# Pair 0's scores among the gate products, roots behind its exponentials, one masked copy per head with differences of value blocks, and another order of the projections

## The chip, the cores and the metric

One core of one Trainium2 chip runs the kernel. The metric is the device time of one execution in microseconds. The kernel before takes 871.64 us (median of three runs, 871.32 to 872.03). Its engines are named as in the profile: PE (TensorE matmuls), PEld (its weight loads), DVE (VectorE), ACT (ScalarE), POOL (GpSimd), SP (SyncE, which here only issues DMAs).

## The reference

One layer of a decoder on 512 tokens of width 1024, all float32: an FFN half step, a mixer, another FFN half step, each with an RMS norm on both sides. The mixer is what matters here.

```python
def rg_lru(x_in, conv_w, conv_b, w_rg, b_rg, w_ig, b_ig, lam):
    xc = causal_depthwise_conv(x_in, conv_w, conv_b)
    r = jax.nn.sigmoid(block_diag(xc, w_rg, b_rg).astype(jnp.float32))
    i = jax.nn.sigmoid(block_diag(xc, w_ig, b_ig).astype(jnp.float32))
    log_a = LRU_C * r * jax.nn.log_sigmoid(lam.astype(jnp.float32))
    a = jnp.exp(log_a)
    mult = jnp.sqrt(-jnp.expm1(2.0 * log_a))
    u = mult * (i * xc.astype(jnp.float32))
...
    _, h = lax.associative_scan(combine, (a, u), axis=1)
...
    scores = jnp.where(mask[None, :, None, None], scores, MASK_VALUE)
    sink = sinks.astype(jnp.float32).reshape(1, 1, N_KV_HEADS, GQA_GROUP, 1, 1)
    m = jnp.maximum(jnp.max(scores, axis=-1, keepdims=True), sink)
    p = jnp.exp(scores - m)
    denom = jnp.sum(p, axis=-1, keepdims=True) + jnp.exp(sink - m)
    p = (p / denom).astype(v.dtype)
    out = jnp.einsum("bnkgqj,bnjkd->bnqkgd", p, v_band)
...
    y_lru = rg_lru(x_lru, conv_w, conv_b, w_rg, b_rg, w_ig, b_ig, lam) * jax.nn.gelu(gate_lru)
    y_attn = sliding_window_sink_attention(q, k, v, sinks)
    y = jnp.concatenate([rms_norm(y_lru, g_lru_out), rms_norm(y_attn, g_attn_out)], axis=-1)
    return y @ w_o
```

The attention has 8 query heads of 64 over 2 key heads, with a window of 128: a query sees its own block of 128 keys up to itself, and of the block before only the keys behind its own place. So for each place in a block exactly one of the two blocks' keys counts, and a head's weights of one query block fit in one 128x128 tile.

## The kernel before

Each float32 product is made of three passes over parts of lower precision: every operand is split into a high part (a cast on ACT) and a low part (a subtraction on DVE), and hi*hi + hi*lo + lo*hi are accumulated in PSUM. Weights are loaded in pieces of 1 MB into five raw buffers (`raw_`) by SP, cast to `whi_` on ACT (line 172) and subtracted to `wlo_` on DVE (line 177). A class `Weights` holds a list of weight units in their order of use. `take` hands out the next one; `cast(n)` puts the casts of the next n on ACT's queue, `fill(n)` their subtractions too, and when a raw buffer's last unit is subtracted the next load goes to SP. The order of all work is the order in which the program text issues it (no scheduler): each engine has one queue and works it off in order, waiting where an operand isn't there.

The program is FFN 1, a boundary (norms and transposes, in which the four products `an` of the recurrence's input are made), the mixer, a second boundary, FFN 2. In the mixer 24 matmuls (eight steps of three) make each further projection: `pk`, `pv`, four `pq` (one per pair of heads; pair j is heads j and j + 4, called n = 0 and 1) and four `gt` (the recurrence's GELU gates). A projection is made in one go by `in_product`, or bit by bit by `pump(n)`, which puts n steps of the next projection in PE's queue between other work.

The recurrence, per 128 of 512 channels (ci = 0 to 3): a convolution (ACT and DVE, `xc`), its split, gate products `rg` and `ig` (six matmuls a ci), sigmoids and tanh (ACT), `decay_a` (exp on ACT, a square `m` on POOL), `decay_b` (DVE), `root` (square root on ACT), `root_u` (a product, on POOL for ci 0 and 1, on DVE for 2 and 3), `scan` (DVE), and at the end a product with the GELU of `gt` (`gelu_a` to `gelu_d`, a copy on DVE, then square and tanh on ACT between DVE steps).

The attention, per pair: `products` (scores `sc` on PE in four PSUM banks, line 1340), `scores` (mask and maximum on DVE, lines 1346 to 1352), `exps` (ACT, line 1361), `normalise` (DVE, line 1368), `turn_p` (transposes on PE, line 1376, a copy `pa` on ACT), masked copies `pc` on POOL (lines 1385 and 1386: for each head four selects, which part a block into its own keys and those of the block before), `values` (products with v on PE, line 1394), `rows_high` and `rows_low` (the split of the result, ACT and DVE). Here pair 0's scores stand behind all gates, pq0, the transposes of v and three steps of pq1; its mask and exponentials stand behind all decays and roots. For j = 1 to 3 a loop puts the values of pair j - 1 in PE's queue, the scores, exponentials and normalisation of pair j on DVE and ACT, five steps of a projection on PE, then pair j's transposes and the scores of pair j + 1.

After the loop the products with w_o follow. Their row scales need the mean squares of both halves (`balance`, which sums on PE the `acc_lru` and `acc_attn` of DVE).

## Time and profile before

| | us |
|---|---|
| median of three runs | 871.64 (871.32 to 872.03) |
| the profiled execution | 869.65, its span 867.9 |
| PE busy | 847.4 (98%) |
| DVE busy | 657.3 (76%) |
| ACT busy | 527.4 (61%) |
| POOL busy | 173.9 (20%) |
| mean granted clock of PE | 0.996 |

The span runs from the first to the last instruction of the profiled execution; the execution's time also has what lies around it. Busy is the sum of an engine's instructions. Matmuls overlap each other, so PE can be busy without being at its peak. A row of a group of instructions names line, engine, operation, output and inputs and shapes, then the count, the busy time in us, the mean of one in ns, and the time that its engine idled before it with what ended the idling.

### The profile page before, as it was taken

What the parts mean: (1) busy time and instruction counts of PE and PEld (TensorE: products, weight loads), DVE (VectorE), ACT (ScalarE), POOL (GpSimd) and SP (SyncE); (2) the same over time, 40 slices, a digit from 0 to 9 for tenths busy, and PEclk for the clock granted to TensorE, in tenths of its full rate; (3) what the DMA queues carried; (4) which work ended last, traced back from release to release, by engine and by line L of the source; (5) the groups of instructions that cost most, each with busy time, mean ns of one, the idle gap of its engine ahead of it and who ended that gap; (6) DMA issues with size and microseconds to landing.
All of it is one profiled execution on the core that took longest, in us unless ns stands there. A gap on an engine that the chain in (4) does not pass through costs nothing.

```text
span 867.9 us, 14095 instructions
## 1 busy us (share of the span) xinstructions
PE 847.4 (98%) x5502; PEld 768.3 (89%) x5502; DVE 657.3 (76%) x898; ACT 527.4 (61%) x896; POOL 173.9 (20%) x211
## 2 busy tenths in 40 slices
...
GB/s 244 98 194 194 146 100 233 178 115 232 116 136 288 125 211 77 91 56 48 82 65 122 64 35 290 74 108 207 120 95 101 237 154 132 233 98 188 262 85 97
DMA packets 92902, 124.42 MB, mean 143 GB/s; under 512 B 5864, under 2 KB 62500, under 8 KB 92836
## 3 DMA queue, kind: packets, MB, share of 16 engines
...
q10 hardware_dynamic: 144, 0.13, 0.0%
...
## 4 chain that ended last, share of the span: by engine, by line
PE 85%; DVE 7%; ACT 4%; DMA 2%; issue 1%; SPq 0%; POOL 0%; DVEq 0%; ACTq 0%
PE aa L820 12%; PE ab L820 11%; PE da L820 6%; PE db L820 5%; PE ba L820 3%; PE wo L1602 3%; PE bb L820 3%; PE an L702 1%; PE mn L702 1%; PE yal L1148 1%; PE yal L1149 1%; PE yal L1147 1%; PE yb L1149 1%; PE yb L1147 1%; PE yb L1148 1%; DMA raw_second<-in_ffn_w_gu 1%
## 5 line engine op out<-in xcount | busy, mean ns | idle before, releaser
L928 POOL DMA_DIRECT2D yp_b<-stage x42 | 36.5, 1111 | 149.7 <-ACT stage L925 144.2
L928 POOL DMA_DIRECT2D yp_a<-stage x42 | 37.0, 1135 | 146.5 <-ACT stage L925 141.2
...
L1147 PE MATMUL yal<-whi_ad,hha 128*128 128x512 f32 x48 | 18.9, 393 | 0.0
L1149 PE MATMUL yal<-whi_ad,hla 128*128 128x512 f32 x48 | 18.7, 390 | 0.0
L1148 PE MATMUL yal<-wlo_ad,hha 128*128 128x512 f32 x48 | 18.7, 389 | 0.0
L1147 PE MATMUL yb<-whi_bd,hhb 128*128 128x512 f32 x48 | 18.7, 389 | 0.0
L1148 PE MATMUL yb<-wlo_bd,hhb 128*128 128x512 f32 x48 | 18.7, 389 | 0.0
L1149 PE MATMUL yb<-whi_bd,hlb 128*128 128x512 f32 x48 | 18.7, 389 | 0.0
L177 DVE TENSOR_TENSOR wlo_bd<-raw_bd,whi_bd 128x1024 fp32r<-128x1024 f32 x10 | 12.1, 1223 | 8.1 <-ACT whi_bd L172 8.1
L1291 POOL TENSOR_TENSOR xcl<-xc,xch 128x512 fp32r<-128x512 f32 x4 | 6.9, 1754 | 54.5 <-ACT xch L1290 54.5
L1385 POOL TENSOR_SCALAR_AFFINE_SELECT pc<-pa 128x256 f32<-128x256 f32 x16 | 10.8, 676 | 32.3 <-ACT pa L1378 32.3
L177 DVE TENSOR_TENSOR wlo_ad<-raw_ad,whi_ad 128x1024 fp32r<-128x1024 f32 x10 | 12.2, 1221 | 4.0 <-ACT whi_ad L172 4.0
L177 DVE TENSOR_TENSOR wlo_wo<-raw_wo,whi_wo 128x1024 fp32r<-128x1024 f32 x8 | 10.0, 1256 | 6.7 <-ACT whi_wo L172 6.5
L1268 DVE SCALAR_TENSOR_TENSOR xc<-an,cols,xc 128x511 f32<-128x511 f32 (+2 forms) x12 | 8.2, 742 | 9.0 <-ACT xc L1264 9.0
L553 POOL TENSOR_TENSOR xg_f<-xh_f,xl_f 128x256 f32<-128x256 f32 x8 | 5.8, 759 | 42.2 <-DVE xl_f L484 42.2
L410 PE MATMUL pq<-xh_mx,whi_q 128*128 128x512 f32 x32 | 13.6, 425 | 0.0
L603 ACT ACTIVATE sqxr<-x_rows 128x512 f32<-128x512 f32 x16 | 10.0, 631 | 5.6 <-DVE x_rows L633 5.6
L1682 POOL TENSOR_TENSOR yp_b<-yp_b,grow 128x512 f32<-128x512 f32 x6 | 7.8, 1292 | 27.2 <-ACT ysq L1675 27.0
L1148 PE MATMUL ybl<-wlo_bd,hhb 128*128 128x512 f32 (+1 forms) x36 | 13.2, 366 | 0.0
L1147 PE MATMUL ybl<-whi_bd,hhb 128*128 128x512 f32 (+1 forms) x36 | 13.2, 366 | 0.0
L1149 PE MATMUL ybl<-whi_bd,hlb 128*128 128x512 f32 (+1 forms) x36 | 13.2, 365 | 0.0
...
## 6 DMA issues: line engine op xcount, KB each, us to landing
...
```

The costliest lines, as they stand in the source:

```text
L177: low.tensor_sub(two(lo, x), x, two(hi.bitcast(F32), x))
L410: pe.matmul(ps, hi[:, k, :], xh, start=start, stop=False)
L603: act.activation(wt(f"sq{name}{self.name}{tb}{dh}"), src, AF.Square, accum_out=self.ss[name, tb][:, dh:dh + 1])
L702: pe.matmul(b[:, l], w[part][:, k, :], xs[k][xpart][:, l], start=k + part + xpart == 0, stop=stop and k == KD - 1)
L820: pe.matmul(o, w[:, k, js], x, start=first and i + j + k == 0, stop=k == 3 and i == 2, skip_group_check=True)
L928: pool.dma_start(o, st.rearrange("p (a b) -> p a b", a=2) if len(o.shape) == 3 else st, accum_op=ALU.add)
L1147: pe.matmul(ps, hh[:, blk], hi[:, k, cs], start=start, stop=False)
L1148: pe.matmul(ps, hh[:, blk], lo[:, k, cs], start=False, stop=False)
L1149: pe.matmul(ps, hl_[:, blk], hi[:, k, cs], start=False, stop=stop)
L1268: dve.scalar_tensor_tensor(o, xl_banks[ci][:, :T - back], col("conv_w", (CONV - 1 - back) * KC + ci), o, op0=ALU.mult, op1=ALU.add)
L1385: pool.affine_select(t[:, :, 0, :], cur, pattern=[[0, 2], [1, P]], base=0, channel_multiplier=-1, compare_op=ALU.is_ge, fill=0.0)
L1602: pe.matmul(wo_banks[tb][dh], x, w[:, k, :], start=start and k == 0 and w is hi and not xp, stop=stop and k == 1 and xp == 1, skip_group_c ...
```

## The change

- Projections are made in another order: pk, pq0, pv, pq1, pq2, gt0, pq3, gt1, gt2, gt3 (before pk, pv, pq0, pq1, gt0, pq2, pq3, gt1, gt2, gt3), and the weights' list and casts follow. All four `conv_a` stand together.
- Pair 0's score products stand between the gate products of ci 1 and ci 2; its mask and maximum follow the gates; then pv, its exponentials, pq1 with the transposes of v inside, its normalisation. `decay_a` comes behind its exponentials, `decay_b` and the roots behind its transposes and the scores of pair 1.
- Per head one select instead of four makes `pc`, of blocks 1 to 3 alone; `pa` stays as the other operand. With vd, the difference of each value block to the one before, a block's own part is pc times vd, and the block behind takes pa times v without a mask. `values` has 12 matmuls instead of 8, for the same columns.
- `root_u` is on DVE for all ci. The copy of `gt` is on ACT instead of DVE, right after its product.
- In the loop a pair's fill is 9, 9 and 10 steps before its transposes instead of 5, and root products, scans and GELU steps stand behind `rows_low`.
- The means (`balance`) come one weight's products later among those of w_o.

PE's queue around pair 0's scores, before (`ig` and `rg` gate products, `vt` the transposes of v, `pq` pq1, `sc` the scores):

```order
L412 MATMUL ig_4490<-xch_4380,lo_w_ig 128x512
L1477 MATMUL vt<-ident,vT 128x128 x4
L410 MATMUL pq_4515<-xh_mx_3694,whi_q_4358 128x512
L411 MATMUL pq_4515<-xl_mx_3695,whi_q_4358 128x512
L412 MATMUL pq_4515<-xh_mx_3694,wlo_q_4359 128x512
L410 MATMUL pq_4515<-xh_mx_3696,whi_q_4358 128x512
L411 MATMUL pq_4515<-xl_mx_3697,whi_q_4358 128x512
L412 MATMUL pq_4515<-xh_mx_3696,wlo_q_4359 128x512
L410 MATMUL pq_4515<-xh_mx_3698,whi_q_4358 128x512
L411 MATMUL pq_4515<-xl_mx_3699,whi_q_4358 128x512
L412 MATMUL pq_4515<-xh_mx_3698,wlo_q_4359 128x512
L1340 MATMUL sc_4526<-kTh,qT0h 128x128
```

and now, where they begin:

```order
L409 MATMUL rg_4433<-xch_4353,lo_w_rg 128x512
L407 MATMUL ig_4434<-xch_4353,hi_w_ig 128x512
L408 MATMUL ig_4434<-xcl_4354,hi_w_ig 128x512
L409 MATMUL ig_4434<-xch_4353,lo_w_ig 128x512
L1338 MATMUL sc_4449<-kTh,qT0h 128x128
L1338 MATMUL sc_4451<-kTh,qT0h 128x128
L1338 MATMUL sc_4449<-kTl,qT0h 128x128
```

The score products stand between two sets of gates (24 score products, then the gates of ci 2 and 3); pv and pq1, 48 matmuls, come behind the second set and ahead of the transposes of pair 0. Before, all gates, the transposes of v and nine matmuls of pq1 stood ahead of them.

DVE's queue between pair 2's normalisation (`sc`) and the low part of pair 3's queries (`qT3l`), which the score products of pair 3 need. Before, pair 2's normalisation is followed by it at once:

```order
L1366 TENSOR_TENSOR den_4931<-den_4931,es_4932 128x4
L1367 RECIPROCAL den_4931<-den_4931 128x4
L1368 TENSOR_TENSOR sc_4933<-sc_4933,den_4931 128x512
L1366 TENSOR_TENSOR den_4947<-den_4947,es_4948 128x4
L1367 RECIPROCAL den_4947<-den_4947 128x4
L1368 TENSOR_TENSOR sc_4949<-sc_4949,den_4947 128x512
L1316 TENSOR_TENSOR qT3l<-pq_4827,qT3h 128x512
L484 SCALAR_TENSOR_TENSOR yal_4956<-po_4914,cols,yah_4955 128x512
```

and now (`yal` and `acc_attn` are pair 1's result and its sum of squares, `xc` the recurrence's input, `gq` its GELU):

```order
L1366 TENSOR_TENSOR sc_4898<-sc_4898,den_4896 128x512
L481 SCALAR_TENSOR_TENSOR yal_4918<-po_4904,cols,yah_4917 128x512
L1410 TENSOR_TENSOR acc_attn<-acc_attn,sq_a_4920 128x512
L1305 TENSOR_TENSOR xc_4314<-xc_4314,th_4489 128x512
L1305 TENSOR_TENSOR xc_4316<-xc_4316,th_4504 128x512
L1308 SCALAR_TENSOR_TENSOR xc_4312<-r_4441,xc_4312 128x512
L1424 SCALAR_TENSOR_TENSOR gq_4860<-gq_4860,gt_4858 128x512
L1314 TENSOR_TENSOR qT3l<-pq_4862,qT3h 128x512
```

Six instructions, two of them root products (`xc<-xc,th`), one a scan (`xc<-r,xc`), stand ahead of the low part.

ACT's queue at the same place, before (`yah` the high part of the result, `pa` the copy of the transposes, `whi_` casts of weights):

```order
L1361 ACTIVATE sc_4949,den_4947<-sc_4866,nm_4945 128x128
L481 ACTIVATE yah_4955<-po_4914,cols 128x512
L441 ACTIVATE sq_a_4958<-po_4914 128x512
L172 CAST whi_wo_4967<-raw_wo_4893 128x1024
L1315 CAST qT3h<-pq_4827 128x512
L1378 COPY pa_4995<-pt_4990 128x512
L1378 COPY pa_5011<-pt_5006 128x512
```

and now:

```order
L1359 ACTIVATE sc_4898,den_4896<-sc_4820,nm_4894 128x128
L478 ACTIVATE yah_4917<-po_4904,cols 128x512
L438 ACTIVATE sq_a_4920<-po_4904 128x512
L172 CAST whi_gt_0_4928<-raw_gt__4846 128x1024
L1427 ACTIVATE gq_4860<-gq_4860 128x512
L1313 CAST qT3h<-pq_4862 128x512
L1376 COPY pa_4975<-pt_4970 128x512
L1376 COPY pa_4987<-pt_4982 128x512
```

The tanh of the first GELU (`gq<-gq`), which needs the DVE step quoted above, stands ahead of the high part `qT3h` and of pair 2's copies.

The diff (cut where it only renames or follows from the rest):

```diff
@@ -306,11 +305,9 @@
-    for add in (q[0], q[1], gt[0], q[2], q[3], *gt[1:]):
+    for add in (kv[0], q[0], kv[1], q[1], q[2], gt[0], q[3], *gt[1:]):
         add()
     WO = [(k, dh) for k in (KC, KC + 2, 0, 2) for dh in range(2)]
 ...
@@ -1257,11 +1254,12 @@
     xcs, th, rs_, us_ = [], [], [], []
-    def conv(c0):
-        for ci in (c0, c0 + 1):
-            xcs.append(t2k(f"xc{ci}"))
-            act.activation(xcs[ci], xl_banks[ci], AF.Identity, bias=col("conv_b", ci), scale=col("conv_w", 3 * KC + ci))
+    def conv_a(ci):
+        xcs.append(t2k(f"xc{ci}"))
+        act.activation(xcs[ci], xl_banks[ci], AF.Identity, bias=col("conv_b", ci), scale=col("conv_w", 3 * KC + ci))
+    def conv_b(c0):
         for back in range(1, CONV):
             for ci in (c0, c0 + 1):
                 o = xcs[ci][:, back:]
@@ -1304,7 +1302,7 @@
         act.activation(th[ci], th[ci], AF.Sqrt)
     def root_u(ci):
-        (pool if ci < 2 else dve).tensor_mul(us_[ci], us_[ci], th[ci])
+        dve.tensor_mul(us_[ci], us_[ci], th[ci])
     def scan(ci):
         dve.tensor_tensor_scan(hl[ci], rs_[ci], us_[ci], initial=0.0, op0=ALU.mult, op1=ALU.add)
@@ -1374,25 +1372,28 @@
         for b in range(NB):
             bs = slice(b * P, (b + 1) * P)
             pe.transpose(pt[:, bs], p[:, bs], ident)
-        pa = wt(f"pa{j}{n}")
+        pa, pc = (t2k(f"{t}{j}{n}") for t in ("pa", "pc"))
         act.copy(pa, pt)
-        pairs = unit[j, n] = [t2k(f"pc{j}{n}{i}") for i in range(2)]
-        for i, t in enumerate(pairs):
-            t = t.rearrange("p (b w k) -> p b w k", b=2, w=2)
-            cur = v4(pa)[:, 2 * i:2 * i + 2, :]
-            pre = v4(pa)[:, 2 * i + 1:min(2 * i + 3, NB), :]
-            nb = 2 - i
-            pool.affine_select(t[:, :, 0, :], cur, pattern=[[0, 2], [1, P]], base=0, channel_multiplier=-1, compare_op=ALU.is_ge, fill=0.0)
-            pool.affine_select(t[:, :nb, 1, :], pre, pattern=[[0, nb], [-1, P]], base=0, channel_multiplier=1, compare_op=ALU.is_gt, fill=0.0)
+        pool.affine_select(v4(pc)[:, 1:, :], v4(pa)[:, 1:, :], pattern=[[0, NB - 1], [1, P]], base=0, channel_multiplier=-1, compare_op=ALU.is_ge, fill=0.0)
+        unit[j, n] = pa, pc
     def values(j):
         o = bank(f"po{j}")
         for b in range(NB):
-            w = P if b == NB - 1 else 2 * P
             for n in range(2):
-                pe.matmul(o[n * HD:(n + 1) * HD, b * P:b * P + w], v[:, b * P + n * HD:b * P + (n + 1) * HD],
-                          unit[j, n][b // 2][:, 2 * (b % 2) * P:2 * (b % 2) * P + w], start=b == 0, stop=b == NB - 1, skip_group_check=True)
+                pa, pc = unit[j, n]
+                chans = slice(b * P + n * HD, b * P + (n + 1) * HD)
+                keys, own = slice(b * P, min(b + 1 + (not b), NB) * P), slice(b * P, (b + 1) * P)
+                if b:
+                    pe.matmul(o[n * HD:(n + 1) * HD, own], vd[:, chans], pc[:, own], start=False, stop=b == NB - 1, skip_group_check=True)
+                else:
+                    pe.matmul(o[n * HD:(n + 1) * HD, keys], v[:, chans], pa[:, keys], start=True, stop=False, skip_group_check=True)
+            for n in range(2):
+                pa, pc = unit[j, n]
+                chans, nxt = slice(b * P + n * HD, b * P + (n + 1) * HD), slice((b + 1) * P, (b + 2) * P)
+                if 0 < b < NB - 1:
+                    pe.matmul(o[n * HD:(n + 1) * HD, nxt], v[:, chans], pa[:, nxt], start=False, stop=False, skip_group_check=True)
         po[j] = o
     def rows_high(j):
@@ -1414,7 +1415,8 @@
     def gelu_a(ci):
         b = gts[ci]
-        gts[ci] = taken(wt(f"gt{ci}"), b)
+        gts[ci] = wt(f"gt{ci}")
+        act.copy(gts[ci], b)
         gqs[ci] = t2k(f"gq{ci}")
         act.activation(gqs[ci], gts[ci], AF.Square, scale=(GC * GA) ** 0.5)
 ...
@@ -1441,12 +1444,11 @@
         yield
     def fill_steps():
-        yield from in_steps("pq1", lambda b: q_parts(1, b), 1)
-        yield from in_steps("gt0", lambda b: gelu(0, b), 0)
-        for j in (2, 3):
-            yield from in_steps(f"pq{j}", lambda b: q_parts(j, b), 0)
+        yield from in_steps("pq2", lambda b: q_parts(2, b))
+        yield from in_steps("gt0", lambda b: gelu(0, b))
+        yield from in_steps("pq3", lambda b: q_parts(3, b))
         for ci in range(1, KC):
-            yield from in_steps(f"gt{ci}", lambda b: gelu(ci, b), 0)
+            yield from in_steps(f"gt{ci}", lambda b: gelu(ci, b))
     steps = fill_steps()
@@ -1454,96 +1456,102 @@
         for _ in range(n):
             next(steps, None)
-    conv(0)
-    pk = in_product("pk", (), 1)
+    for ci in range(KC):
+        conv_a(ci)
+    conv_b(0)
+    pk = in_product("pk", (), 0)
     split_xc(0)
     split_xc(1)
-    W.cast(3)
-    conv(2)
-    W.fill(2)
+    conv_b(2)
+    pq = in_product("pq0", (), 0)
+    W.cast(1)
     kT = in_parts(pk, "kT")
+    W.cast(2)
     split_xc(2)
     split_xc(3)
-    pv = in_product("pv", (), 2)
-    vT = taken(wt("vT"), pv)
+    preload(AF.Sigmoid)
+    q_parts(0, pq)
+    W.fill(2)
     lru_gates(0)
     lru_gates(1)
-    pq = in_product("pq0", (), 2)
+    products(0)
     lru_gates(2)
     lru_gates(3)
-    q_parts(0, pq)
-    vt = bank("vt")
-    for b in range(NB):
-        pe.transpose(vt[:, b * P:(b + 1) * P], vT[:, b * P:(b + 1) * P], ident)
-    v = t2k("v")
-    dve.tensor_copy(v, vt)
-    pump(3)
-    products(0)
-    preload(AF.Exp)
-    for ci in range(KC):
-        decay_a(ci)
-    for ci in range(KC):
-        decay_b(ci)
-    preload(AF.Sqrt)
-    for ci in range(KC):
-        root(ci)
+    for n in range(2):
+        scores(0, n)
+    pv = in_product("pv", (), 0)
     W.cast(2)
     preload(AF.Exp)
     for n in range(2):
-        scores(0, n)
         exps(0, n)
-    W.fill(2)
-    for n in range(2):
-        normalise(0, n)
-    pump(5)
+    vT = taken(wt("vT"), pv)
+    vt = bank("vt")
+    def turn_v():
+        for b in range(NB):
+            pe.transpose(vt[:, b * P:(b + 1) * P], vT[:, b * P:(b + 1) * P], ident)
+    pq = in_product("pq1", {2: turn_v}, 0)
+    normalise(0, 0)
+    v, vd = t2k("v"), t2k("vd")
+    dve.tensor_copy(v, vt)
+    normalise(0, 1)
+    W.fill(1)
     for ci in range(KC):
-        root_u(ci)
-    SPLIT = W.taken + 3
-    beside = {0: [(scan, 0), (gelu_a, 0)], 1: [(scan, 1), (gelu_b, 0), (gelu_c, 0)], 2: [(gelu_d, 0)], 3: [(gelu_a, 1), (gelu_b, 1), (gelu_c, 1)]}
-    for j in range(KC):
-        if j:
-            values(j - 1)
+        decay_a(ci)
+    q_parts(1, pq)
+    dve.tensor_sub(vd[:, P:], v[:, P:], v[:, :T - P])
+    turn_p(0, 0)
+    pump(1)
+    turn_p(0, 1)
+    products(1)
+    W.cast(1)
+    preload(AF.Sqrt)
+    for ci in range(KC):
+        decay_b(ci)
+        root(ci)
+    W.fill(1)
+    preload(AF.Exp)
+    pump(4)
+    after = {0: [(root_u, 0), (root_u, 1), (scan, 0)],
+             1: [(root_u, 2), (root_u, 3), (scan, 1), (gelu_b, 0), (gelu_c, 0)],
+             2: [(scan, 2), (gelu_d, 0), (gelu_b, 1), (gelu_c, 1)]}
+    for j in range(KC - 1):
         for n in range(2):
-            if j:
-                scores(j, n)
-                exps(j, n)
-        if j:
-            rows_high(j - 1)
-            W.fill(SPLIT + 2 * j - W.taken)
+            scores(j + 1, n)
+            exps(j + 1, n)
+        values(j)
+        rows_high(j)
+        W.fill(1)
         for n in range(2):
-            if j:
-                normalise(j, n)
-            else:
-                scan(2 + n)
-        if j == 0:
-            W.fill(SPLIT - W.taken)
-        W.cast(SPLIT + 2 * j + 1 - W.taken)
-        pump(5 if j else 8)
-        turn_p(j, 0)
+            normalise(j + 1, n)
+        W.cast(2)
+        rows_low(j)
+        for fn, i in after[j]:
+            fn(i)
+        pump((9, 9, 10)[j])
+        turn_p(j + 1, 0)
         pump(1)
-        turn_p(j, 1)
-        if j < KC - 1:
-            products(j + 1)
-        if j:
-            rows_low(j - 1)
-        W.fill(SPLIT + 2 * j + 1 - W.taken)
-        W.cast(SPLIT + 2 * j + 2 - W.taken)
-        for fn, i in beside[j]:
-            fn(i)
+        turn_p(j + 1, 1)
+        if j < KC - 2:
+            products(j + 2)
+        W.fill(2)
         pump(4)
+    W.cast(3)
+    scan(3)
+    gelu_b(2)
+    gelu_c(2)
+    gelu_d(1)
+    pump(100)
     values(3)
     rows_high(3)
     rows_low(3)
-    gelu_d(1)
-    gelu_a(2)
-    gelu_b(2)
-    gelu_c(2)
-    pump(100)
-    gelu_a(3)
+    W.fill(3)
+    W.cast(4)
     gelu_b(3)
     gelu_c(3)
+    W.fill(4)
     accl = tmp.tile([P, T], F32, tag="acc", name="acc_lru", bufs=1)
@@ -1616,8 +1624,10 @@
             for k0, dh in WO[:2]:
                 for tb in range(NB - 1):
                     wo_product(tb, dh, k0, False, False, (1,))
+            W.fill(2)
+        if n == 2:
             balance()
-            W.fill(4)
+            W.fill(3)
         if n >= 2:
             for tb in range(NB - 1):
                 rescale(tb, dh)
```

14 lines of the change are left out of this document (6 added, 8 removed).

## The prediction

> **What bounds the kernel now.** I read the page's head first, then the windows (busy time of each engine in a stretch), then the waits of PE, then the timeline inside the mixer.
>
> ```profile
> span 867.9 us, 14095 instructions
> ```
>
> In a windows row the first figure is the stretch's length, then come the busy us of PE, PEld, DVE, ACT, POOL, the granted clock and the DMA.
>
> ```profile
> 0.00:377.34 377.34, 374.67 (x2570) 349.79 (x2571) 303.39 (x421) 236.60 (x379) 63.62 (x81) 1.00 0.59 163
> 377.34:494.70 117.36, 107.12 (x574) 83.81 (x573) 86.02 (x144) 77.02 (x169) 47.14 (x50) 0.99 0.23 59
> 494.70:867.90 373.20, 365.64 (x2362) 334.70 (x2360) 267.85 (x334) 213.73 (x348) 63.09 (x80) 1.00 0.53 150
> ```
>
> PE is the bound: it is idle for 2.67 + 10.24 + 7.56 = 20.5 us of the span. The change touches the middle row alone, from the first product after the boundary (pk) to where the second boundary starts. There PE idles 117.36 - 107.12 = 10.24 us, half of it all; the rows on either side are PE work nearly end to end. The stretch, cut where the idle lies:
>
> ```profile
> 412.80:417.60 4.80, 0.00 (x0) 0.03 (x1) 4.52 (x14) 4.79 (x22) 0.00 (x0) 1.00 0.01 2
> 417.60:422.47 4.87, 4.87 (x36) 4.02 (x36) 4.84 (x7) 3.97 (x6) 2.36 (x3) 0.65 0.01 3
> 422.47:425.43 2.96, 2.96 (x14) 2.17 (x12) 2.96 (x4) 0.00 (x0) 2.96 (x3) 1.00 0.00 0
> 425.43:428.66 3.23, 2.31 (x17) 1.24 (x16) 3.16 (x6) 0.63 (x1) 2.13 (x4) 1.00 0.95 200
> 428.66:433.71 5.05, 3.70 (x17) 2.77 (x16) 4.74 (x14) 3.94 (x20) 0.00 (x0) 1.00 1.06 207
> 433.71:440.75 7.04, 6.52 (x47) 5.07 (x47) 5.87 (x9) 4.20 (x8) 4.55 (x7) 1.00 0.46 81
> 440.75:446.79 6.04, 5.36 (x33) 3.83 (x32) 5.69 (x17) 4.23 (x21) 0.50 (x2) 1.00 0.38 146
> 446.79:453.82 7.03, 6.51 (x47) 5.03 (x48) 5.86 (x10) 3.85 (x7) 4.54 (x8) 1.00 0.01 2
> 453.82:463.91 10.09, 9.80 (x56) 7.30 (x55) 9.27 (x21) 7.67 (x25) 2.49 (x6) 1.00 0.34 110
> 463.91:466.51 2.60, 2.50 (x18) 1.15 (x17) 0.84 (x1) 0.99 (x2) 2.60 (x5) 1.00 0.86 221
> 470.06:481.14 11.08, 10.13 (x53) 8.38 (x52) 8.15 (x11) 7.69 (x13) 4.25 (x3) 1.00 0.00 1
> 481.14:494.70 13.56, 13.56 (x62) 11.22 (x62) 6.80 (x10) 8.48 (x14) 0.00 (x0) 1.00 0.03 4
> ```
>
> ```profile
> PE pt L1376 <- DVE den L1366: 6.8, 3, 4.8
> PE po L1394 <- POOL pc L1386: 0.9, 1, 0.9
> ```
>
> The reader is to see two things. In the 4.80 us DVE (4.52) and ACT (4.79) are both full: PE stands before the transposes of pair 0 until scores, exponentials and normalisation are through, and these stood behind the recurrence's roots. And after it PE works at a granted clock of 0.65.
>
> **The change, part by part.** What goes away, against PE working through:
>
> - the wait before pair 0's transposes, 4.80. The scores of pair 0 now start behind two of the four gate products, with two gates, pv and pq1 still ahead of the transposes;
> - the slow clock behind it: 4.87 x (1 - 0.65) = 1.70;
> - pair 0's value products, which waited for POOL's selects. Undisturbed they take 442.42 - 440.75 = 1.67 (rows below), here 3.23: 1.56;
> - the wait of pair 1's transposes, 5.05 - 3.70 = 1.35, and the same in the next rows: 0.52, 0.68, 0.52, 0.29. In these the subtraction of a weight stood between scores and normalisation, and the fill ahead of the transposes was five steps; it is now nine or ten, and the subtraction stands elsewhere;
> - pair 3's value products, 2.60 - 1.67 = 0.93;
> - the wait for the squares of the recurrence before the means, 11.08 - 10.13 = 0.95: one more weight's products now stand ahead.
>
> Together 13.30 us.
>
> ```profile
> 377.34 0.40 PE L410 MATMUL pk<-xh_mx,whi_kv 128*128 128x512 f32 x1
> 382.81 0.39 PE L410 MATMUL pv<-xh_mx,whi_kv 128*128 128x512 f32 x1
> 436.42 0.33 PE L1340 MATMUL sc<-kTh,qT2l 64*128 64x128 f32 x2 [0.29 <-DVE qT2l L1316]
> 437.81 0.50 PE L410 MATMUL pq<-xh_mx,whi_q 128*128 128x512 f32 x1
> 440.75 1.73 PE L1394 MATMUL po<-pc,v 128*64 128x256 f32 x16
> 442.42 0.50 PE L410 MATMUL pq<-xh_mx,whi_q 128*128 128x512 f32 x1
> 459.47 0.63 PE L1376 MATMUL pt<-ident,sc 128*128 128x128 f32 x4 [0.29 <-ACT yah L481]
> 460.98 0.48 PE L410 MATMUL gt<-xh_mx,whi_gt 128*128 128x512 f32 x1
> 427.25 0.41 DVE L1346 COPY_PREDICATED sc<-up,sc 128x256 f32<-128x256 uint8 x1
> 433.88 0.69 DVE L1368 TENSOR_TENSOR sc<-sc,den 128x512 f32<-128x512 f32 x1
> ```
>
> A product of 24 matmuls takes 382.81 - 377.34 = 5.47, so one of its eight steps 0.684. From the end of one pair's score products to the next pair's, PE now has four steps (2.96, the 422.47 row), the value products (1.67), nine steps (9 x 0.684 = 6.16) and the transposes with a step between (460.98 - 459.47 = 1.51): 12.30 us. Against this stands the queue of DVE and ACT:
>
> ```profile
> L177 DVE TENSOR_TENSOR wlo_q<-raw_q,whi_q 128x1024 fp32r<-128x1024 f32 x4 | 5.5, 1375 | 0.0
> L1310 DVE TENSOR_TENSOR_SCAN xc<-r,xc 128x512 f32<-128x512 f32 x4 | 5.4, 1376 | 0.0
> L1307 DVE TENSOR_TENSOR xc<-xc,th 128x512 f32<-128x512 f32 x2 | 1.3, 680 | 0.0
> L484 DVE SCALAR_TENSOR_TENSOR yal<-po,cols,yah 128x512 fp32r<-128x512 f32 x4 | 3.0, 744 | 2.7 <-ACT sq_a L441 2.7
> L1409 DVE TENSOR_TENSOR acc_attn<-acc_attn,sq_a 128x512 f32<-128x512 f32 x3 | 2.3, 762 | 0.0
> L1422 DVE SCALAR_TENSOR_TENSOR gq<-gq,gt 128x512 f32<-128x512 f32 x4 | 4.5, 1137 | 2.1 <-ACT gq L1419 2.1
> L1316 DVE TENSOR_TENSOR qT3l<-pq,qT3h 128x512 fp32r<-128x512 f32 x1 | 0.7, 690 | 1.0 <-ACT qT3h L1315 1.0
> L1425 ACT ACTIVATE gq<-gq 128x512 f32<-128x512 f32 x4 | 2.5, 632 | 6.8 <-DVE gq L1422 6.8
> L1315 ACT CAST qT3h<-pq 128x512 fp32r<-128x512 f32 x1 | 0.6, 622 | 0.0
> ```
>
> Scores to the end of normalisation took 433.88 + 0.69 - 427.25 = 7.32 before, with a subtraction of 1.22 in it that mostly lay in ACT's time; without it I take 6.7.
>
> *Pair 2's score products.* After qT1l DVE does the difference of value blocks (0.5, an estimate: 3/4 of 0.68), four decay products at 0.68, a subtraction of 1.375: 4.6, of which 1.8 lie beside pair 1's score products (an estimate from the 1.39 below and the part that needs no low half). So scores start 2.8 after these; 6.7 more to the end of normalisation; then, new, ahead of qT2l: yal 0.74, two root products 1.36 (one pair of them was POOL's), a scan 1.38, and qT2l itself 0.69. Sum 13.7 against 12.30: PE waits 1.4, less 0.2 of matmuls that need only the high half: 1.2.
>
> *Pair 3's.* Two subtractions (2.75) stand behind qT2l, and PE runs 437.81 - 436.42 = 1.39 of score products beside them: scores start 1.36 late. Then 6.7, yal 0.74, sum of squares 0.76, two root products 1.36, scan 1.38, the GELU step on DVE 0.8 (the 1137 ns holds two stretched ones). ACT's tanh waits for that step, and qT3h stands behind the tanh in ACT's queue: 0.63 + 0.62, then qT3l 0.69. Sum 15.0 against 12.30: 2.7, less 0.2: 2.5. This is the largest new wait: behind the tanh also stand pair 2's two copies and behind qT3l two subtractions.
>
> *Pair 3's values and the means.* The copies for POOL's last select stand behind a tanh, a copy and a square. Bounds 0 and the 1.56 of pair 0 before; I take 0.6. For the means bounds 0 and 0.95; 0.2, as DVE ends about there.
>
> *The shape of the value products.* Twelve instead of eight, with the same columns (256 + 5 x 128 against 3 x 256 + 128, each for two heads). Bounds: nothing, and by the number of instructions 4 x 1.67 x 0.5 = 3.3. I take 0.3, since each still stands next to the other head's, as before.
>
> ```profile
> L1385 POOL TENSOR_SCALAR_AFFINE_SELECT pc<-pa 128x256 f32<-128x256 f32 x16 | 10.8, 676 | 32.3 <-ACT pa L1378 32.3
> 436.20 0.41 POOL L1385 TENSOR_SCALAR_AFFINE_SELECT pc<-pa 128x256 f32<-128x256 f32 x1 [8.64 <-ACT pa L1378]
> L1307 POOL TENSOR_TENSOR xc<-xc,th 128x512 f32<-128x512 f32 x2 | 3.4, 1748 | 0.0
> ```
>
> *At nothing.* The selects: 32 become 8 of 1.5 times the size, about 1.0 each, covered by the four steps (2.96); uncovered, two would cost 2.0 a pair. Four GELU copies go from DVE to ACT, which is busy 77.02 of 117.36; with no slack there they would add some 0.6 each. Two root products go from POOL (1.75 each) to DVE (0.68 each); they are in the queue above. Weights: each now has one product of cover, 5.47, against a rounding and a subtraction on two engines; SP's later loads (gates, then w_o) follow the subtractions that free their buffers and are asked for more than 10 us after.
>
> New waits: 1.2 + 2.5 + 0.6 + 0.2 + 0.3 = 4.8. **Gain 13.3 - 4.8 = 8.5 us.** The profiled execution took 869.65 (span 867.9), 2 us under the median of the three runs, 871.64; the gain is taken off either: 861.2 for such an execution, **863.1** for the median.
>
> By the Trainium skill, "TensorE: Matmul & The Clock Gate", section "HAM oscillation — how this bites in real kernels", PE is to have no idle gap over some 3.4 us, or its clock halves. The rows agree as far as they go: 0.65 behind 4.80 of idle, 1.00 behind 1.35. By the rule the new wait of 2.5 costs no clock and the sum stays; without it, bounded by these two rows, up to 1.70 more, 864.8.
>
> The selects took 676 ns in the mean, and 0.41 where DVE left them alone (the 436.20 row). By the Trainium skill, "SBUF — State Buffer", section "Who interferes with whom", a DVE instruction with two SBUF inputs and a POOL instruction that reads SBUF shut each other out for a whole instruction; the two figures fit that, and it speaks against the change, which puts root products, scans and subtractions on DVE beside the selects. By the rule the last select, the only one with little cover, could wait a whole scan (1.38): 864.5, inside the forecast's range.
>
> **The rivals.**
>
> *The new queue costs nothing* (20%). The DVE rows above are means that hold stretched instructions, and PE's fill may run slower than 0.684 a step after each switch; then only about 0.5 remains: 871.64 - 13.3 + 0.5 = 858.8. Against it: the chain for pair 3 has 15.0 us of rows in one line.
>
> *The new waits are dearer* (15%). Value products paced by their number (+3.0) and the slow clock once more (+1.7): 863.1 + 4.7 = 867.8. For it: 1.70 was lost that way before.
>
> *Slower: DVE becomes the bound of the loop* (5%). It is one queue from products to products, 15.0 of rows against 12.3 + 1.4 on PE; every tenth more on DVE's rows is 1.5 in each of three loops and the tail, 6 in all. From 14% more it is slower than before; at 20%, 863.1 + 12 = 875. For it: the GELU step's mean of 1137 ns. Against: POOL, beside whose work the stretched ones lay, loses three quarters of its selects.
>
> *It moves and does not go* (4%). The last w_o weights come late behind the longer DVE queue and PE waits there for what it won: 871. Against: the last of the windows rows, from the means to the second boundary, shows no idle, and the weights keep their distance to it.
>
> **How the numbers follow.** Forecast 56%. The range 858.5 to 867.5 holds it and the cheap case and reaches to the dear one. About 0.2% (1.7 us) can be told from no change; the first three cases are all faster by more: 0.91; within: 0.04; slower: 0.05.
>
> **What would show it.** Right: no idle before pair 0's transposes and a clock of 1.00 throughout; PE at the first w_o product some 8 us earlier; one wait of 2 to 3 us of pair 3's score products on qT3h and qT3l, a smaller one on qT2l; value products of 1.7. Wrong: any wait of PE over 3 us, a clock under 1.00 behind a wait, the transposes still waiting for normalisation, or idle PE on weights behind the means.

## The result, and the profile after

| | before | changed |
|---|---|---|
| median, us (lowest to highest) | 871.73 (871.32 to 872.03) | 860.30 (859.08 to 861.45) |
| executions | 4 | 4 |
| the profiled execution, us (span) | 869.65 (867.9) | 860.56 (858.5) |

The ratio is 0.9869 with a 95% interval of 0.9852 to 0.9886. The forecast was 863.1 with a range of 858.5 to 867.5: the gain was forecast as 8.5 us and is 11.4 between the medians, 9.1 between the two profiled executions. Why these two differ is part of what follows.

The windows of the changed kernel, cut as before: up to the first product after the boundary, the mixer, and from the start of the second boundary (in a row: length, busy us of PE, PEld, DVE, ACT, POOL, the granted clock, DMA).

```profile
0.00:377.33 377.33, 375.08 (x2570) 350.13 (x2571) 303.37 (x421) 237.35 (x380) 63.49 (x81) 1.00 0.58 160
377.33:485.39 108.06, 106.52 (x607) 86.43 (x606) 86.05 (x143) 78.67 (x174) 28.54 (x24) 0.97 0.27 75
485.39:858.50 373.11, 365.29 (x2360) 334.43 (x2358) 267.43 (x334) 213.60 (x348) 62.99 (x80) 1.00 0.53 150
```

All of it went in the middle row: 117.36 us became 108.06, 9.30 less; the other two rows are as they were within 0.1 us. PE idles 1.54 us there instead of 10.24. But the granted clock of the stretch is 0.97, where it was 0.99, and that is one of the signs by which the forecast was to be wrong (a clock under 1.00 behind a wait). The waits of PE that remain in it:

```profile
PE sc L1338 <- DVE qT2l L1314: 1.3, 1, 1.3
...
PE rms_mix L1587 <- DVE acc_lru L1563: 0.3, 1, 0.3
```

No wait before the transposes of any pair is left, and none on POOL's selects. Pair 2's score products wait for the low part of the queries, as the forecast said and for about as long as it said (1.2; how, the account below shows); the larger wait that it gave to pair 3's score products (2.5) is not there at all. The rows where the clock falls:

```profile
421.07:425.81 4.74, 3.47 (x36) 2.85 (x34) 4.74 (x7) 3.05 (x5) 1.93 (x2) 1.00 0.00 0
425.81:430.00 4.19, 4.19 (x13) 3.34 (x12) 3.99 (x11) 2.32 (x8) 0.00 (x0) 0.59 0.67 145
...
471.87:474.05 2.18, 1.91 (x17) 1.91 (x17) 1.55 (x3) 2.17 (x5) 0.00 (x0) 0.95 0.91 278
474.05:477.20 3.15, 3.15 (x9) 2.47 (x10) 3.12 (x8) 3.15 (x7) 0.00 (x0) 0.50 0.82 276
```

Twice PE works at half clock (a granted clock of 0.50) for some 3.5 us: behind the wait of pair 2 (1.27 us of idle in the 4.74), and behind the sixteen one-column matmuls of the means (2.18 us with 0.27 of idle). In the timeline of PE, the transposes, the value products of pair 0 and the first product with w_o:

```profile
406.88 0.60 PE L1374 MATMUL pt<-ident,sc 128*128 128x128 f32 x4
413.09 0.65 PE L1391 MATMUL po<-pa,v 128*64 128x256 f32 x4
414.76 0.50 PE L407 MATMUL pq<-xh_mx,whi_q 128*128 128x512 f32 x1
459.30 0.50 PE L1610 MATMUL wo<-whi_wo,yah 128*128 128x512 f32 x1
```

Value products take 414.76 - 413.09 = 1.67 us, to the hundredth what eight undisturbed matmuls took before. The first w_o product stands at 459.30, 10.8 us earlier (forecast some 8).

### The profile page after: what moved, and what is told of

It is laid out like the page before. It is cut to its first block, busy times and chain, and to the rows that moved or that the text cites. A ratio compares the mean times of both kernels' runs of the same rounds, so it can differ in the third digit from the quotient of the medians.

```text
span 858.5 us, 14132 instructions
## 1 busy us (share of the span) xinstructions
PE 846.9 (99%) x5534; PEld 771.0 (90%) x5534; DVE 656.8 (77%) x897; ACT 529.6 (62%) x901; POOL 155.0 (18%) x185
## 4 chain that ended last, share of the span: by engine, by line
PE 89%; DVE 5%; ACT 3%; DMA 1%; issue 1%; SPq 0%; DVEq 0%; ACTq 0%
PE aa L817 12%; PE ab L817 11%; PE da L817 6%; PE db L817 5%; PE ba L817 3%; PE bb L817 3%; PE wo L1610 3%; PE mn L699 1%; PE an L699 1%; PE yal L1144 1%; PE yal L1146 1%; PE yb L1144 1%; PE yb L1146 1%; PE yal L1145 1%; PE yb L1145 1%; DMA raw_second<-in_ffn_w_gu 1%
## 5 line engine op out<-in xcount | busy, mean ns | idle before, releaser
L1289 POOL TENSOR_TENSOR xcl<-xc,xch 128x512 fp32r<-128x512 f32 x4 | 5.1, 1292 | 52.3 <-ACT xch L1288 52.3
L1610 PE MATMUL wo<-whi_wo,yah 128*128 128x512 f32 x32 | 13.7, 428 | 0.0
L1377 POOL TENSOR_SCALAR_AFFINE_SELECT pc<-pa 128x384 f32<-128x384 f32 x8 | 6.2, 784 | 41.6 <-ACT pa L1376 41.6
L407 PE MATMUL gt<-xh_mx,whi_gt 128*128 128x512 f32 x32 | 13.3, 416 | 0.0
L1610 PE MATMUL wo<-wlo_wo,yah 128*128 128x512 f32 x32 | 13.3, 414 | 0.0
```

The costliest lines, as they stand in the source:

```text
L407: pe.matmul(ps, hi[:, k, :], xh, start=start, stop=False)
L1377: pool.affine_select(v4(pc)[:, 1:, :], v4(pa)[:, 1:, :], pattern=[[0, NB - 1], [1, P]], base=0, channel_multiplier=-1, compare_op=ALU.is_g ...
L1610: pe.matmul(wo_banks[tb][dh], x, w[:, k, :], start=start and k == 0 and w is hi and not xp, stop=stop and k == 1 and xp == 1, skip_group_c ...
```

## The experiments

Three questions were open: why pair 3's wait is missing, what half clock has to do with the size of the gain, and which parts of the change carry it. All medians; the ratio is to the kernel before, run beside each group, whose medians were 871.19 to 871.65:

| kernel | median, us | lowest to highest | ratio to before (95%) |
|---|---|---|---|
| before, once more | 872.39 | 869.50 to 873.58 | 1.0013 (1.0002 to 1.0024) |
| changed, once more | 859.96 | 859.18 to 860.93 | 0.9878 (0.9860 to 0.9896) |
| roots first | 868.98 | 867.80 to 870.67 | 0.9975 (0.9965 to 0.9986) |
| old selects | 860.20 | 859.91 to 860.65 | 0.9878 (0.9864 to 0.9893) |
| short fill | 867.76 | 867.61 to 868.89 | 0.9965 (0.9952 to 0.9978) |
| value blocks alone | 870.31 | 868.70 to 873.03 | 0.9989 (0.9977 to 1.0001) |
| root products on POOL | 859.90 | 858.91 to 861.20 | 0.9874 (0.9857 to 0.9892) |
| queries first | 859.49 | 858.37 to 862.03 | 0.9868 (0.9851 to 0.9885) |
| means split | 858.47 | 858.27 to 858.64 | 0.9850 (0.9837 to 0.9864) |
| both of these | 857.63 | 857.22 to 858.65 | 0.9843 (0.9828 to 0.9857) |
| subtractions first | 857.67 | 857.56 to 857.76 | 0.9848 (0.9833 to 0.9863) |
| means late | 857.55 | 857.31 to 857.98 | 0.9836 (0.9822 to 0.9850) |

### The kernel before, once more

No edit.

> The kernel before, unchanged, for the granted clock of several executions. In its first profile a stretch of 3.5 us runs at half clock behind the 4.80 us gap, and that execution took 869.65 us, 2.0 less than the median of the timed ones. If half-clock stretches make the scatter: each stretch more costs about 1.7 us (3.5 us at half speed), executions near 871.7 show a mean clock lower by 0.002 (0.994) than the one at 869.65 (0.996). If something else makes it: the same clock at different spans.

Ten executions, ordered by mean clock: 869.50 at 0.995; 871.59 and 871.69 at 0.993; 871.86 and 872.03 at 0.991; 872.75 to 873.58 at 0.989 and 0.990. The twenty executions of the kernel before that ran beside it lie on the same steps. Its trace (mean clock 0.989) shows where:

```profile
415.10:422.70 7.60, 4.81 (x27) 4.11 (x29) 7.43 (x14) 6.72 (x21) 2.30 (x3) 0.55 0.01 3
480.20:487.70 7.50, 7.50 (x26) 6.30 (x27) 5.33 (x9) 3.37 (x7) 0.00 (x0) 0.54 0.00 1
```

Half clock for 6.8 us at the gap of pair 0 (it starts in the gap; PE works for 4.8 of it), and for 6.8 behind the means; the profile that the forecast went by had 3.4 at the first place and none at the second. At half speed that is 0.5 x (4.81 + 6.8 - 3.4) = 4.1 us more, less 0.6 that pair 0's selects then wait less, against 3.5 between the two executions. So the scatter between these two is half clock, and 869.65 was one of the fastest executions that this kernel has. It also says how far medians can be trusted here: the same text against itself came out 0.13% apart.

### The changed kernel, once more

No edit.

> The changed kernel, unchanged, for more executions of it and a second trace. If the scatter comes from half-clock stretches alone, its executions lie at 861.4 (mean clock 0.993), 860.3 (0.995) and 859.1 (0.997) as the first four did, and below 859 at 0.998 or 0.999. If the wait of pair 3's score products is only hidden by half clock ahead of it, a trace without a half-clock stretch between 422 and 430 us shows 0.8 us on qT3h and 0.28 us on qT3l, and one with it shows none.

Two executions at 0.999 took 859.18 and 859.24, not less than 859 as expected; two at 0.995 took 860.69 and 860.93. The trace is of the first; its waits, three of its windows and the first transposes of the second boundary:

```profile
PE sc L1338 <- DVE qT2l L1314: 1.3, 1, 1.3
PE sc L1338 <- ACT qT3h L1313: 0.8, 1, 0.8
...
PE rms_mix L1587 <- DVE acc_lru L1563: 0.5, 1, 0.5
...
PE sc L1338 <- DVE qT3l L1314: 0.3, 1, 0.3
```

```profile
422.00:424.70 2.70, 1.48 (x11) 0.98 (x10) 2.70 (x5) 2.44 (x4) 1.73 (x2) 1.00 0.00 0
...
426.12:430.00 3.88, 3.88 (x28) 2.96 (x28) 3.71 (x10) 2.01 (x6) 0.00 (x0) 1.00 0.64 145
...
474.30:477.40 3.10, 3.10 (x15) 2.57 (x15) 3.07 (x8) 3.10 (x6) 0.00 (x0) 1.00 0.84 286
```

```profile
497.44 1.22 PE L648 MATMUL tp_r<-ident,xn_r 128*128 128x128 f32 x8
```

The same wait of pair 2 as in the first trace (1.27 us), a longer one before the means (0.45 for 0.27), and full clock behind both. And now pair 3's score products do wait: 0.79 on qT3h and 0.29 on qT3l, 1.08 together, just as expected of a trace without half clock. In the first trace PE, which had worked at half clock, took 14.18 us from the end of pair 2's score products (425.81) to there instead of 12.66 (426.12 to the wait), and found the queries ready. Up to the first product behind pair 3's scores the two traces take 15.78 us (425.81 to 441.59) and 15.54 (426.12 to 441.66). So the forecast's mechanism holds, its size does not, and the wait and the half clock stand in for each other. Behind the means nothing absorbs the half clock: from there to the transposes of the second boundary the first trace takes 57.19 us, the second 55.78.

From pk's first product to those transposes (`tp_r`) PE does the same work in each kernel but for the value products. This stretch is used below where a median cannot tell: 131.13 us before (377.34 to 508.47), 121.45 in the first trace, 119.80 in the second (377.64 to 497.44).

The mean clock of an execution says less than the expectation made of it. In the trace of root products on POOL (below, 859.10 at 0.997) the clock is 1.00 in the whole stretch (120.08 us), as it is here at 0.999. The two differ behind the last product: PE is busy there for some 0.7 of the last 8 us, at a clock of 0.67 there and 0.85 here.

### Roots first

Decays and roots of the recurrence go back ahead of pair 0's mask and exponentials; the rest stays changed.

```diff
+    preload(AF.Exp)
+    for ci in range(KC):
+        decay_a(ci)
+    for ci in range(KC):
+        decay_b(ci)
+    preload(AF.Sqrt)
+    for ci in range(KC):
+        root(ci)
     for n in range(2):
         scores(0, n)
     pv = in_product("pv", (), 0)
```

> The changed kernel with one thing undone: decays and roots of the recurrence again ahead of pair 0's mask and exponentials; scores among the gates, the order of projections, the selects and the fill stay. Theory 1 (the 4.80 us gap came from the queue of DVE and ACT, not from too little PE work): decays need ACT 2.6 and 2.2 us, two table loads 3.0, DVE 3.1; pair 0's normalisation, which ends 1.6 us ahead of the second head's transposes in the changed kernel, ends some 5 to 6 us later; PE waits 3.5 to 4.5 us before the transposes, and a half-clock stretch follows (1.7): 864 to 866 us. Rival (the scores' place among the gates and pv behind them are enough cover): no wait over 1 us, 860 to 861 us.

868.98, 8.7 us more than the changed kernel and worse than expected. The wait in its trace, and DVE's timeline there:

```profile
PE vt L1500 <- DVE vT L1252: 8.1, 1, 8.1
```

```profile
401.60 5.00 DVE L1299 SCALAR_TENSOR_TENSOR th<-m,th 128x512 f32<-128x512 f32 x4 [7.58 <-POOL m L1296]
406.53 0.42 DVE L1344 COPY_PREDICATED sc<-up,sc 128x256 f32<-128x256 uint8 x1
...
410.62 0.69 DVE L1252 COPY vT<-pv 128x512 f32<-128x512 f32 x1
```

DVE stands idle for 7.58 us, because the decays at the head of its queue need POOL's squares of ACT's exponentials, and these stand behind the sigmoids and tanh of all gates in ACT's queue; the mask of pair 0, whose scores are long there, starts at 406.53 (in the changed kernel 393.03). The copy of pv stands behind the mask, and so PE waits already before the transposes of v, earlier than expected. This one edit is worth more than the whole gap of before. In this kernel what it mends is an idle DVE, not a busy one; in the kernel before DVE stood idle for 1.96 us ahead of the decays, and was then busy with them for 6.12.

### Old selects

`turn_p` and `values` as before (four selects a head, eight value matmuls, no difference of value blocks).

> The changed kernel with the old masked copies and value products (four selects a head, eight value matmuls), everything else as changed. Theory 1 (forecast: the value products no longer wait on POOL's selects, worth 1.56 + 0.93 us against the kernel before): each pair's value products wait again, 0.5 to 1.5 us for pairs 0 and 3, nothing for the others, and take 1.67 us undisturbed, as with twelve matmuls; 861.5 to 862.5 us. Rival (the four steps and the other order hide the selects anyway): no wait on the selects, 860 to 860.5 us, and the difference of value blocks is worth nothing here.

860.20, no difference that the medians can tell: the theory's time is missed. The trace (clock 0.996, no half clock in the mixer):

```profile
PE po L1392 <- POOL pc L1384: 1.9, 3, 0.9
...
PE sc L1338 <- ACT qT3h L1313: 0.9, 1, 0.9
```

The waits on the selects come, as the theory said: 1.9 us in three places (0.32 for pair 0, 0.73 and 0.89 for pair 3). But pair 2's wait of 1.27 is gone in return. The difference of value blocks is itself a step of DVE, ahead of everything that pair 2's queries stand behind, and took 1.15 us in the changed kernel (the forecast had 0.5):

```profile
408.43 1.15 DVE L1503 TENSOR_TENSOR vd<-v 128x384 f32<-128x384 f32 x1
```

With full clock in both, the masked copies do pay: the stretch from pk to `tp_r` takes 121.21 us in this trace and 119.80 in the changed kernel's second. Pair 3's value products alone take 4.14 (457.67 to 461.81) instead of 1.68. The changed kernel's median hides this: five of its eight executions have mean clocks of 0.995 or less, none of this kernel's four. At 0.999 the one takes 859.18 and 859.24, the other 859.91.

### Value blocks alone

The same part on the kernel before: `turn_p` and `values` of the change, and the subtraction for `vd` behind the copy of v.

> The kernel before with the masked copies and value products of the change alone (one select a head, differences of value blocks, twelve matmuls). Theory 1 (the forecast's terms): the waits on POOL's selects before pair 0's and pair 3's value products (0.92 and 0.68 us) are gone, and the value products take 1.67 us each; 869.5 to 870.4 us against 871.4. Rival (the difference of value blocks stands in the one full queue, DVE's, ahead of pair 0's transposes or pair 1's scores, and gives it back): 871 to 872 us.

870.31 against 871.53: inside the first theory's range, but the interval just holds 1, and the trace holds two half-clock stretches, so neither theory is clear by the time. By the trace both are half right:

```profile
425.93 0.65 PE L1393 MATMUL po<-pa,v 128*64 128x256 f32 x4
...
433.60 0.63 PE L1376 MATMUL pt<-ident,sc 128*128 128x128 f32 x4 [2.30 <-DVE den L1366]
```

The value products begin at once (pair 3's take 1.68). But the transposes of pair 1, which waited 1.35 before, now wait 2.30: they start at 433.60, and started at 433.71 before, when DVE has the normalisation; what PE won at the value products it spent in front of the next thing that DVE owed it.

### Short fill

```diff
-        pump((9, 9, 10)[j])
+        pump((6, 7, 6)[j])
```

The nine steps run behind the loop, and with them the second gate's GELU steps.

> The changed kernel with 6, 7 and 6 steps of fill ahead of the transposes instead of 9, 9 and 10; the nine steps taken away run behind the loop (the second gate's GELU steps with them, which need them). Theory 1 (the queue of DVE and ACT from one pair's scores to the next sets the loop, and the fill covers it): PE stands before the transposes of pairs 1 to 3 or the scores behind them for 2.0, 1.4 and 2.7 us more than now, together 5 to 6 us, with one half-clock stretch at least: 865 to 867 us. Rival (the fill merely moved): no new wait over 0.5 us, 860 to 861 us.

```profile
PE sc L1338 <- ACT qT3h L1313: 3.4, 1, 3.4
PE sc L1338 <- DVE qT2l L1314: 1.8, 1, 1.8
...
PE sc L1338 <- ACT qT2h L1313: 0.6, 1, 0.6
...
PE pt L1374 <- DVE sc L1366: 0.5, 1, 0.5
```

867.76: 7.5 us more, a little over the theory's bound. These waits are 6.4 us (with two small ones 7.3, against 2.8 in the changed kernel's second trace), mostly not before the transposes but one step later, at the queries; there are two half-clock stretches beside them. So the longer fill is what covers DVE's queue, and it is worth nearly as much as the order of pair 0. Order and fill do not add up: undone apart they cost 8.7 and 7.5, and the whole change won 11.4.

### Root products on POOL

```diff
-        dve.tensor_mul(us_[ci], us_[ci], th[ci])
+        (pool if ci < 2 else dve).tensor_mul(us_[ci], us_[ci], th[ci])
```

> The changed kernel with the root products of ci 0 and 1 back on POOL. Theory 1 (DVE's queue to qT2l is what pair 2's score products wait for; two root products are 1.28 us of it, and POOL is idle there for 11 us): the 1.27 us wait goes to 0 to 0.3 us, the selects of pair 1 are not delayed, the wait of pair 3's stays; 858.8 to 859.8 us. Rival (POOL's two products of 1.75 us each and DVE's steps beside them slow each other, as the stretched DVE steps of the first trace suggest): DVE's steps of that stretch lengthen by 1 us or more, the wait stays over 0.8 us; 860 to 861 us.

859.90, unchanged (0.1 under the rival's range, 0.1 over the theory's); by the trace it is the rival. Of this kernel's timeline, and of the changed kernel's second trace:

```profile
412.41 3.66 POOL L1305 TENSOR_TENSOR xc<-xc,th 128x512 f32<-128x512 f32 x2 [1.47 <-ACT th L1302]
412.61 2.31 DVE L177 TENSOR_TENSOR wlo_gt<-raw_gt__4416,whi_gt 128x1024 fp32r<-128x1024 f32 x1
```

```profile
412.88 1.21 DVE L177 TENSOR_TENSOR wlo_gt<-raw_gt__4416,whi_gt 128x1024 fp32r<-128x1024 f32 x1
```

DVE is rid of 1.28 us of products, and the subtraction that runs beside them on POOL takes 1.10 longer. Pair 2's score products wait 0.63 on the high part and 0.64 on the low part of their queries, the same 1.27 as without the edit. The forecast had charged the two moved products to DVE's queue as new; on POOL they cost it nearly as much.

### Queries first

The recurrence's steps of the loop stand behind the next pair's score products, not ahead of its queries.

```diff
         rows_low(j)
-        for fn, i in after[j]:
-            fn(i)
         pump((9, 9, 10)[j])
...
         if j < KC - 2:
             products(j + 2)
+        for fn, i in after[j]:
+            fn(i)
         W.fill(2)
```

> The changed kernel with the recurrence's steps of the loop (root products, scans, GELU steps) put behind the next pair's score products instead of ahead of its queries, on DVE and ACT. Theory 1 (the waits of pair 2's and pair 3's score products come from these steps ahead of qT2l, qT3h and qT3l, and the half clock from the first wait): the 1.27 us wait on qT2l, the wait on qT3h (1.1 and 0.9 us in the traces with roots first and with the old selects, none in the changed kernel's) and the half-clock stretch behind them are gone; 857.0 to 858.3 us against 860.3. Rival (DVE has no room in the loop: the same 4 to 5 us of steps then delay the next pair's scores): a wait of 1 to 2 us before the transposes of pair 2 or 3 takes their place; 859.5 to 860.5 us.

```profile
PE pq L409 <- DVE wlo_q L177: 1.2, 1, 1.2
PE rms_mix L1587 <- DVE acc_lru L1563: 0.7, 1, 0.7
```

859.49: between the theories, and no difference that the medians can tell (858.37 to 862.03). At full clock its trace takes 118.72 us from pk to `tp_r`, 1.1 less than the changed kernel's. The waits on qT2l, qT3h and qT3l are gone, so the steps ahead of them were the cause. In their place PE waits 1.18 for a subtracted weight, which now stands behind those steps: not at the transposes, as the rival said, but for the reason that it gave.

### Means split

The eight matmuls for the attention's squares stand one weight's products ahead of the recurrence's eight.

```diff
+        if n == 1:
+            mean(1)
         if n == 2:
+            mean(0)
             balance()
```

> The changed kernel with the 16 one-column matmuls of the means no longer in a row: the eight for the attention's squares stand one weight's products earlier. Theory 1 (the granted clock falls to half for some 3.5 us when PE had little to do within a stretch of about that length, idle or with tiny matmuls): no half-clock stretch behind the means any more, which the changed kernel's trace shows for 3.15 us after 474.05; 858.6 to 859.6 us. Rival (the clock falls by unbroken idle time only): 0.27 us of idle before the means stays as it is, the half-clock stretch with it; 860.0 to 860.6 us.

858.47, 1.8 less than the changed kernel (1.5 less than its second median), and four executions within 0.4 us of each other at clocks of 0.997 to 0.999. There is no half clock behind the means in its trace:

```profile
469.00:476.50 7.50, 7.50 (x38) 6.31 (x37) 6.62 (x13) 7.41 (x13) 0.00 (x0) 1.00 0.98 341
```

From pk to `tp_r` it takes 119.19 us, 0.6 less than the changed kernel at full clock: about the wait before the means (0.45), which is gone as well. The rest of the gain in the median goes with the half clock. As the wait went with the split, the run does not by itself tell tiny matmuls from idle time; 0.27 us of idle is little to set against 1.9 us of matmuls of one column.

### Both, subtractions first, means late

Both edits together; then also the two subtractions of weights ahead of the recurrence's steps; then also the means behind the third and fourth weights of w_o, with all rescalings.

```diff
+        W.fill(2)
         for fn, i in after[j]:
             fn(i)
-        W.fill(2)
```

```diff
-        if n == 1:
-            mean(1)
         if n == 2:
+            mean(1)
+            W.fill(3)
+        if n == 3:
             mean(0)
             balance()
-            W.fill(3)
-        if n >= 2:
-            for tb in range(NB - 1):
-                rescale(tb, dh)
+            for dh in range(2):
+                for tb in range(NB - 1):
+                    rescale(tb, dh)
```

> The two edits before (recurrence's steps behind the next pair's score products, means in two places) in one kernel. Theory 1: no wait over 0.5 us and no half-clock stretch between the first boundary and the second; 855.5 to 857.0 us. Rival: one of the waits comes back at the transposes, with its half-clock stretch; 858.5 to 860 us.

> The kernel with both edits, and the two subtractions of weights that stood behind the recurrence's steps put ahead of them, right behind the score products. Theory 1 (the 1.17 us wait of pq3's first step on wlo_q came from the steps put ahead of it): that wait is gone, none over 0.4 us is left in the mixer and no half-clock stretch; 856.0 to 856.8 us against 857.6. Rival (DVE has no room: scores of pair 2 start as late as before, and the wait moves to its transposes): a wait of 0.8 to 1.2 us on normalisation; 857.3 to 858 us.

> The kernel with both edits and the subtractions first, and the means one more weight's products later (the attention's eight matmuls behind the third weight's products of w_o, the recurrence's behind the fourth's), all rescalings behind them. Theory 1 (with the subtractions first DVE's steps only ended later, and the means wait 0.45 and 0.96 us for its last sums): the means wait for nothing, no wait over 0.4 us is left between the boundaries; 856.0 to 856.8 us against 857.67. Rival (what depends on the means is late next: six rescalings on ACT and the next norm's first block): the waits on the means are gone, and a wait on the rescaled banks or the next boundary takes as much; 857.3 to 858.2 us.

857.63, 857.67 and 857.55: three kernels, one time. The waits of PE between the boundaries in each of the three traces:

```profile
PE pq L409 <- DVE wlo_q L177: 1.2, 1, 1.2
```

```profile
PE rms_mix L1587 <- DVE acc_lru L1563: 1.0, 1, 1.0
...
PE rms_mix L1587 <- DVE acc_attn L1410: 0.4, 1, 0.4
```

```profile
PE wo L1614 <- DVE wlo_wo L177: 1.3, 1, 1.3
```

Each edit removed the wait that it aimed at, and 1.2 to 1.4 us came up at the next thing that DVE delivers. The first came out between its theory and its rival, the last two in their rivals' ranges, the wait at another place than the rivals named: before the means, and at a subtracted weight of w_o. In every one of the three DVE is what is waited for, and none of the three orders of its queue gave the rest back. DVE is not busy throughout (12.4 of the 15 us from 440 to 455 in the trace of subtractions first); most of its idle time there is a wait for ACT, so it is the chain over both queues that is late.

These kernels are 2.3 to 2.8 us better than the changed one by medians. Between traces with full clock, from pk to `tp_r`, the split of the means gives 0.6 us, queries first 1.1, and the three kernels 2.0, 1.6 and 1.7 (117.82, 118.17 and 118.12 for 119.80); the rest of the medians' difference is half clock.

## Why the prediction was right, and where it was wrong

Set against the second trace of the changed kernel, which has no half clock in the mixer, the forecast's sum reads (what was removed has no measurement of its own: it is the rows of before, taken as gone):

| term, us | forecast | measured |
|---|---|---|
| stalls removed: gap of pair 0, its half clock, selects, transposes, queries, means | -13.30 | -13.30, from the rows of before |
| pair 2's score products | +1.2 | +1.27 |
| pair 3's score products | +2.5 | +1.08 |
| pair 3's values | +0.6 | 0 |
| means | +0.2 | +0.45 |
| shape of the value products | +0.3 | 0 |
| sum | -8.5 | -10.50 |

The two profiled executions stand 869.65 - 859.18 = 10.47 apart, but that this meets the sum is in part luck. From pk to `tp_r` the gain is 131.13 - 119.80 = 11.33, and 0.8 of it belongs to no term of the sum; outside this stretch the execution of the second trace takes 0.9 more (pk starts 0.30 later in it). PE's idle time in the stretch fell from 10.24 to 2.80. The waits before the transposes and the value products are gone, those on queries and before the means are in the terms below the first, and the direction and the mechanism were right.

Two of the four small rows that the forecast counted as waits before transposes (0.52 and 0.52) are something else: pair 2's and pair 3's score products, which in the kernel before wait 0.23 and 0.29 us for the high and the low part of their queries (the 436.42 row shows the second). So these waits are not new in the changed kernel, they grew; the sum is right, as it takes away the old ones and adds the new.

Pair 2's term came out at 1.27 for 1.2 since its errors nearly cancel. The chain in the second trace:

```profile
410.46 0.50 PE L407 MATMUL pq<-xh_mx,whi_q 128*128 128x512 f32 x1
414.01 0.41 DVE L1344 COPY_PREDICATED sc<-up,sc 128x256 f32<-128x256 uint8 x1
421.03 0.75 DVE L481 SCALAR_TENSOR_TENSOR yal<-po,cols,yah 128x512 fp32r<-128x512 f32 x1
424.75 0.33 PE L1338 MATMUL sc<-kTh,qT2l 64*128 64x128 f32 x2 [1.27 <-DVE qT2l L1314]
```

Scores start 3.55 us late (forecast 2.8: the difference of value blocks took 1.15, not 0.5) and the whole chain takes 14.29 (13.7). But PE took 12.58 (12.30) to the queries, and had 0.44 (0.2) of products of the high part. Three things were wrong.

**The term of pair 3's score products was mis-sized.** The step was "Sum 15.0 against 12.30: 2.7, less 0.2: 2.5". The same chain in the second trace:

```profile
426.12 0.50 PE L407 MATMUL gt<-xh_mx,whi_gt 128*128 128x512 f32 x1
427.04 0.42 DVE L1344 COPY_PREDICATED sc<-up,sc 128x256 f32<-128x256 uint8 x1
434.11 0.75 DVE L481 SCALAR_TENSOR_TENSOR yal<-po,cols,yah 128x512 fp32r<-128x512 f32 x1
438.42 0.63 ACT L1427 ACTIVATE gq<-gq 128x512 f32<-128x512 f32 x1 [3.47 <-DVE gq L1424]
439.55 0.69 DVE L1314 TENSOR_TENSOR qT3l<-pq,qT3h 128x512 fp32r<-128x512 f32 x1 [1.17 <-ACT qT3h L1313]
439.57 0.33 PE L1338 MATMUL sc<-kTh,qT3h 64*128 64x128 f32 x2 [0.79 <-ACT qT3h L1313]
440.30 0.33 PE L1338 MATMUL sc<-kTh,qT3l 64*128 64x128 f32 x2 [0.29 <-DVE qT3l L1314]
```

From the end of one pair's score products (426.12) to qT3l (440.30) are 14.18 us, where the forecast added 15.04. Scores start 0.92 late (forecast 1.36) and take 7.07 to the result's low part (6.7); that step, the sum of squares, two root products, scan and GELU step take 438.42 - 434.11 = 4.31 (5.04). The sum was made of group means, and these hold longer instructions that ran beside POOL's work (the scan 1376 ns in the mean, here 1.22 us; the sum of squares 762, here 0.68); and instructions that follow each other on DVE start some 0.08 us before the one ahead has ended by its own duration (yal at 434.11 lasts 0.75, the next starts at 434.78). PE's side was 12.66 (439.57 - 0.79 - 426.12; forecast 12.30), and another 0.44 lay beside products of the high part alone (0.2). That is 0.86 + 0.36 + 0.24 = 1.46 less, and 1.08 is left of 2.5. The rival in which the new queue costs nothing named two of these reasons, the means and PE's slower side; the truth lies between it and the forecast.

**The clock was held to fall only behind a long gap.** The forecast read 0.65 behind 4.80 us of idle and 1.00 behind 1.35, and said that it would be 1.00 throughout. In the first trace it fell behind 1.27 us, and behind the means; in the second trace behind neither, with the same wait of pair 2 and a longer one before the means. By the Trainium skill, "TensorE: Matmul & The Clock Gate", section "What's actually happening", the clock follows what PE did within a free-running window of about 3.4 us. The runs agree. The half-clock stretches in the mixer last 3.4 or 6.8 us, and their starts within one trace lie a whole number of 3.41 us apart: 426.07 and 473.85 in the first trace of the changed kernel (47.78, 14 times), 415.82 and 480.67 in the second of the kernel before (64.85, 19 times). So where a wait falls in such a window can differ from execution to execution, and the same work at the same place got half clock in some and not in others. In the first trace one window, from 422.65 to 426.06, holds the whole wait of pair 2; in the second, by the start of its half clock behind the last product (854.60, less 126 times 3.413, an estimate), a boundary falls at 424.5, inside the wait.

The rule that the forecast quoted from the same page of the Trainium skill, section "HAM oscillation — how this bites in real kernels" (no idle gap over some 3.4 us), is too lax for this kernel. Here are the 3.4 us up to the first half clock in the changed kernel's first trace; the same in root products on POOL, as placed by the edges of its half clock behind the last product (an estimate); and in the kernel before the window ahead of the one after which half clock came:

```profile
422.65:426.06 3.41, 2.14 (x27) 1.79 (x26) 3.41 (x5) 1.53 (x2) 1.93 (x2) 1.00 0.00 0
...
421.65:425.06 3.41, 2.13 (x18) 1.39 (x18) 3.41 (x5) 3.41 (x6) 0.94 (x2) 1.00 0.00 0
...
411.18:414.59 3.41, 1.62 (x8) 1.00 (x6) 3.20 (x10) 3.38 (x8) 0.88 (x1) 1.00 0.00 0
```

Only the first was followed by half clock at once, with 1.27 us of idle; the second had 1.28, the third 1.79. So idle time alone does not decide. The first window is the only one of these that holds all 24 short score products, which fits that they count for less than products of 512 columns; what counts, and how much of it keeps the clock, no run settles.

The half clock costs less than it seems where a wait follows: 15.78 us against 15.54, as shown above. Behind the means nothing follows to absorb it.

**The base was one execution of a kernel that has several times.** The forecast took its 8.5 off both the profiled execution and the median. But most executions of before have more half clock than the profiled one: 871.2 to 872.1 at clocks of 0.991 to 0.993, against 869.65. Its median lies 2.1 us above that execution, the changed kernel's 1.1 above its second trace; this 1.0 is what stands between 10.5 and 11.4. The forecast had no term for it. That half clock went with the gap before pair 0 fits the traces, which show none there any more, but only two executions of each kernel were traced.

Of the parts costed at nothing, no wait of PE in the two traces ends on a select or on a GELU copy; no run has the copies undone alone. The difference of value blocks, costed at 0.5, is 1.15 us of DVE, and without it (old selects) pair 2's wait was gone. So of the waits on selects that the masked copies remove, part came back there: they bring 1.4 us at full clock, and nothing by the medians. The forecast had the root products in this wait with 1.36; putting them back on POOL did not shorten it. That DVE's and POOL's instructions lengthen each other (the Trainium skill, "SBUF — State Buffer", section "Who interferes with whom") is borne out on DVE's side: 1.21 us became 2.31 beside POOL's products. What the forecast made of it, a wait on the last select, did not happen.

The rival in which DVE becomes the bound of the loop (5%, "slower") was right about the place: in the kernels built on the changed one, the waits that were removed came back in part at something that DVE delivers (but for the wait that the split of the means took away). It was wrong about the height: the rows of pair 3's chain are not 20% dearer than the forecast had them, but 6% cheaper.

Not tested alone, so that their share stays open: pair 0's score products among the gates, the new order of the projections, the later means and the GELU copies.
